# Splitting the second half of the last image pair's load by partitions into 8 and 120, in a 3x3 convolution on one core

## Chip, cores and metric

One core of one Trainium2 chip. The metric is device time in microseconds (us) per execution. The kernel before has a median of 127.45 us over 3 runs (127.39 to 127.47). In the profile, PE is the matrix engine (TensorE), PEld its weight loads, DVE the vector engine, ACT the scalar engine, POOL is GpSimd, SP is the queue that issues the stores and, at the start, the loads of the weights and of the first rows.

## The reference

```
x:      (16, 64, 64, 64) float32       # batch, channels in, rows, columns
weight: (128, 64, 3, 3)  float32       # nine tenths zeros, drawn at random
out[b, co] = sum over ci, kh, kw of weight[co, ci, kh, kw] * x_pad[b, ci, kh:kh+64, kw:kw+64]
```

It is a plain 3x3 convolution with padding 1; the kernel treats the weights as dense.

## The kernel before

The 16 images are taken as 8 pairs: two images of 64 channels fill the 128 partitions. GpSimd loads each pair from memory and casts it to bf16 on the way. SP stores the float32 results.

```python
xs = [x_pool.tile([128, H, W], BF16, name=f"x{p}") for p in range(NP)]      # one tile for each pair
nc.sync.dma_start(out=w_sb, in_=...)                                       # weights, SP's queue
nc.sync.dma_start(out=x_head, in_=pair(0)[:, 0:HEAD, :])                   # first rows of pair 0
nc.gpsimd.dma_start(out=xs[0][:, HEAD:H, :], in_=pair(0)[:, HEAD:H, :])    # load 0 on GpSimd
ident = const_pool.tile([128, 128], BF16, name="ident"); make_identity(nc, ident)
for p in range(1, NP):
    nc.gpsimd.dma_start(out=xs[p], in_=pair(p))                            # loads 1 to 7

for _ in range(27):                                                        # idle matmuls, wake the clock
    nc.tensor.matmul(idle_ps, idle_rhs, idle_rhs, start=True, stop=True)
# ... weights transposed ...

def twos(p, o, r0):                          # 16 rows; needs a sum of row pairs, made on GpSimd
    s = s_pool.tile([128, 8, W], BF16, name="s")
    nc.gpsimd.tensor_tensor(out=s, in0=xs[p][:, r0 : r0 + 16 : 2, :],
                            in1=xs[p][:, r0 + 1 : r0 + 16 : 2, :], op=ADD)
    shared = product([(s, G1, 0, 1)], 8)     # PE, in program order: s first, then x
    # ... even and odd rows: product(...) of xs[p], added to shared on DVE ...

for p in range(NP):
    # ... block 0 of pair 0 goes the direct way (no s), all other blocks through twos ...
    # ... two stores of 2 MB for each pair; four of 1 MB for the last pair ...
```

GpSimd's queue is one sequence. The loads stand on it first, then all the block sums s. PE needs one s for each block, in order.

Of the kernel before, what the change touches and what calls it, by code (L numbers as in the profile page):

```python
# [27 lines left out]
def kernel(  # L28
# [6 lines left out]
    nc = tc.nc  # L35

    B, C_IN, H, W = x.shape
    C_OUT, _, KH, KW = weight.shape
    assert (B, C_IN, H, W) == (16, 64, 64, 64) and (C_OUT, KH, KW) == (128, 3, 3)
    NP = B // 2  # L40
# [14 lines left out]
    def pair(p):  # L55
        return x[2 * p : 2 * p + 2].rearrange("n i h w -> (n i) h w")

    xs = [x_pool.tile([128, H, W], BF16, name=f"x{p}") for p in range(NP)]
# [4 lines left out]
    nc.gpsimd.dma_start(out=xs[0][:, HEAD:H, :], in_=pair(0)[:, HEAD:H, :])  # L63
    ident = const_pool.tile([128, 128], BF16, name="ident")
    make_identity(nc, ident)
    for p in range(1, NP):
        nc.gpsimd.dma_start(out=xs[p], in_=pair(p))  # L67


    idle_rhs = const_pool.tile([128, 128], BF16, name="idle_rhs")  # L70
# [147 lines left out]
```

## Time and profile before

| | before |
|---|---|
| time, median | 127.45 us |
| profiled execution, span | 125.7 us |
| first store issued | 24.06 us |
| pair 6's first store issued | 100.84 us |
| last store: first, median, second last, last of its 16 landings | 121.84, 122.72, 123.76, 124.56 us |

The last two rows come from the trace's records. In the trace each transfer raises its semaphore 16 times, as many times as the core has DMA engines, and the time of every rise is recorded. This text reads each rise as the landing of one engine's share, so one transfer's 16 landings show how far the engines are apart. The records don't carry the engine's number.

The profile's page of the kernel before. The rows of digits cut the span into 40 slices: PE, POOL and DMA are tenths of busy time, PEclk the clock granted to PE.

```profile
span 125.7 us, 2486 instructions
...
PE   6689999999999999999999999999999999990000
...
POOL 6908543333333333333333333333333330000000
PEclk9999999999999999999999999999999999997555
DMA  4999999999999999999999999999999999999980
...
PE 84%; DMA 4%; DVE 1%; issue 1%; DVEq 0%; SPq 0%
```

PE is full in every slice from the fourth until its work ends near 113 us, and DMA from the second slice until the last stores drain. The last line, the chain that ended last, is 84% PE. It ends with DVE's last additions at 114.2 us; what follows is the drain of the stores. Two limits nearly tie: PE feeds the stores, and the DMA engines carry a backlog to the end.

Stages of the kernel before. The columns are busy time of PE, PEld, DVE, ACT and POOL with instruction counts, then granted clock, DMA share and GB/s.

```profile
90.00:100.00 10.00, 10.00 (x96) 5.15 (x94) 7.82 (x13) 3.22 (x6) 3.45 (x3) 1.00 0.99 423
100.00:110.00 10.00, 10.00 (x98) 5.08 (x94) 7.96 (x14) 3.22 (x6) 1.15 (x1) 1.00 1.02 434
110.00:120.00 10.00, 2.86 (x28) 1.27 (x24) 3.48 (x6) 1.07 (x2) 0.00 (x0) 0.75 0.98 410
```

DMA has no room left. The start, as a timeline of the kernel before (start, duration, engine, line, operation; in brackets the idle time before it and what ended it):

```profile
6.68 6.89 PE L134 MATMUL ps<-x,wT 64*128 64x512 bf16 x36 [1.21 <-DVE x L87]
10.00 3.37 POOL L153 TENSOR_TENSOR s<-x 128x512 bf16<-128x512 bf16 x3 [3.81 <-DMA x<-in_x_dram]
13.39 0.82 PE L134 MATMUL ps<-s,wT 64*128 64x512 bf16 x6
```

GpSimd starts the sums at 10.00 us, just after load 0's last landing (9.86 us). PE reaches the first product of s at 13.39 us and finds it ready: no bracket, so no wait.

### The profile page before, as it was taken

The numbers are of one execution on the slowest core, as the hardware profiler recorded it, in microseconds if no ns is written. First come the engines' busy times: TensorE is split into PE (matmuls) and PEld (weight loads), VectorE is DVE, ScalarE is ACT, GpSimd is POOL, SyncE is SP. The second block draws the span as 40 slices with busy tenths as digits, with TensorE's granted clock in tenths as the row PEclk, the third lists the DMA queues.
The fourth block names the chain that finished last, engine by engine and source line by source line (L and its number), as shares of the span: only waits on it lengthen the run. The fifth ranks groups of instructions, "written<-read, shape, count | busy, mean of one in ns | idle before, by whom it ended". The sixth has DMA issues, their size and how long they took to land.

```text
span 125.7 us, 2486 instructions
## 1 busy us (share of the span) xinstructions
PE 110.5 (88%) x1002; PEld 57.5 (46%) x1002; DVE 82.2 (65%) x135; ACT 38.1 (30%) x70; POOL 40.7 (32%) x45
## 2 busy tenths in 40 slices
PE   6689999999999999999999999999999999990000
PEld 6434555555555455545554555555555555540000
DVE  0452277788878787877787778777877787773000
ACT  4511533333333333332433333333333333330000
POOL 6908543333333333333333333333333330000000
PEclk9999999999999999999999999999999999997555
DMA  4999999999999999999999999999999999999980
GB/s 116 254 220 214 219 216 216 214 203 334 313 292 334 334 302 344 323 318 352 412 435 433 433 433 422 417 438 425 443 422 422 412 438 427 448 396 407 422 362 21
DMA packets 4044, 42.70 MB, mean 340 GB/s; under 512 B 448, under 2 KB 448, under 8 KB 832
## 3 DMA queue, kind: packets, MB, share of 16 engines
q1 hardware_dynamic: 2880, 34.44, 65.6%
q0 software_dynamic: 1152, 8.09, 31.3%
q8 instruction: 8, 0.13, 0.4%
q14 instruction: 4, 0.03, 0.1%
HBM read 17.07 MB, written 33.55 MB: 403 GB/s over the span
## 4 chain that ended last, share of the span: by engine, by line
PE 84%; DMA 4%; DVE 1%; issue 1%; DVEq 0%; SPq 0%
PE ps L134 84%; DMA x_head<-in_x_dram 4%; DVE o L167 1%; DVEq L213 0%; DVE x L87 0%; SPq L60 0%; DVEq L167 0%
## 5 line engine op out<-in xcount | busy, mean ns | idle before, releaser
L134 PE MATMUL ps<-x,wT 64*128 64x504 bf16 (+3 forms) x780 | 91.5, 382 | 1.2 <-DVE x L87 1.2
L167 DVE TENSOR_TENSOR o<-ps,pc 128x512 f32<-128x512 f32 x124 | 77.8, 685 | 22.1 <-PE ps L134 19.8
L134 PEld LDWEIGHTS <-wT 64*128 64x128 bf16 x966 | 53.9, 96 | 53.3 <-issue 4.5
L153 POOL TENSOR_TENSOR s<-x 128x512 bf16<-128x512 bf16 x31 | 35.6, 1151 | 60.2 <-PE ps L134 42.9
L160 ACT COPY pc<-ps 128x512 f32<-128x512 f32 x62 | 33.3, 589 | 64.0 <-issue 61.8
L134 PE MATMUL ps<-s,wT 64*128 64x512 bf16 (+1 forms) x186 | 25.6, 377 | 0.0
L148 DVE COPY o<-ps 128x512 f32<-128x512 f32 x2 | 1.4, 691 | 4.9 <-PE ps L134 4.9
L74 PE MATMUL ps<-idle_rhs 128*128 128x128 bf16 x27 | 3.1, 313 | 1.0 <-DVE idle_rhs L71 1.0
L67 POOL DMA_DIRECT2D x<-in_x_dram x7 | 3.7, 561 | 0.0
L74 PEld LDWEIGHTS <-idle_rhs 128*128 128x128 bf16 x27 | 2.8, 148 | 1.0 <-DVE idle_rhs L71 1.0
L147 ACT COPY o<-ps 128x512 f32<-128x512 f32 x2 | 1.2, 586 | 6.2 <-PE ps L134 6.2
L91 DVE CAST w_bf<-w_sb 128x192 bf16<-128x192 f32 (+1 forms) x4 | 1.1, 353 | 2.8 <-DMA w_sb<-in_weight_dram 2.8
L91 ACT ACT_TABLE_LOAD x1 | 1.3, 1283 | 0.7 <-PEq L202 0.7
L97 PE MATMUL ps<-ident,w_bf 128*128 128x128 bf16 x9 | 1.2, 309 | 0.2 <-DVE w_bf L91 0.2
L87 DVE CAST x<-x_head 128x576 bf16<-128x576 f32 x1 | 0.5, 459 | 1.3 <-DMA x_head<-in_x_dram 1.3
L91 ACT CAST w_bf<-w_sb 128x64 bf16<-128x64 f32 (+1 forms) x2 | 0.7, 420 | 1.7 <-DMA w_sb<-in_weight_dram 1.7
L97 PEld LDWEIGHTS <-w_bf 128*128 128x128 bf16 x9 | 0.8, 129 | 0.6 <-DVE w_bf L91 0.6
L101 DVE TENSOR_TENSOR wT<-ps,wT 128x384 bf16<-128x384 f32 x2 | 1.0, 546 | 0.0
L63 POOL DMA_DIRECT2D x<-in_x_dram x1 | 0.7, 696 | 0.8 <-POOLq L202 0.8
L87 ACT CAST x<-x_head 128x576 bf16<-128x576 f32 x1 | 0.7, 672 | 0.2 <-DMA x_head<-in_x_dram 0.2
L71 DVE MEMSET idle_rhs<- 128x64 uint32 x1 | 0.1, 112 | 0.8 <-PEq L202 0.8
L110 ACT CAST wT<-ps 128x384 bf16<-128x384 f32 x1 | 0.5, 478 | 0.4 <-PE ps L97 0.4
(8 smaller groups left out, 1.9 us busy)
## 6 DMA issues: line engine op xcount, KB each, us to landing
out_dram<-o SPq DMA_DIRECT2D x14, 2048.0 KB, 17.9
x<-in_x_dram POOLq DMA_DIRECT2D x7, 1024.0 KB, 29.9
out_dram<-o SPq DMA_DIRECT2D x4, 1024.0 KB, 10.2
x<-in_x_dram POOLq DMA_DIRECT2D x1, 736.0 KB, 8.6
x_head<-in_x_dram SPq DMA_DIRECT2D x1, 576.0 KB, 5.0
w_sb<-in_weight_dram SPq DMA_DIRECT2D x1, 288.0 KB, 2.9
```

The costliest lines, as they stand in the source:

```text
L67: nc.gpsimd.dma_start(out=xs[p], in_=pair(p))
L74: nc.tensor.matmul(idle_ps, idle_rhs, idle_rhs, start=True, stop=True)
L87: copy(out=xs[0][:, a:b, :], in_=x_head[:, a:b, :])
L91: copy(out=w_bf4[:, g, a:b, :], in_=w_v[:, k : k + b - a, :])
L97: nc.tensor.matmul(wps[:, j, :], src, ident, start=True, stop=True)
L101: nc.vector.tensor_tensor(out=wT[:, g], in0=wps, in1=wT[:, G1], op=SUB)
L134: nc.tensor.matmul(ps[n][:, lo:hi, c_lo:c_hi], tap(g, kw, n), src[q, a:b:step, c_lo + kw - 1 : c_hi + kw - 1], start=(i == 0), stop=(i == ...
L147: nc.scalar.copy(out=o[0][:, r0 : r0 + rows, :], in_=ps[0])
L148: nc.vector.tensor_copy(out=o[1][:, r0 : r0 + rows, :], in_=ps[1])
L153: nc.gpsimd.tensor_tensor(out=s, in0=xs[p][:, r0 : r0 + 16 : 2, :], in1=xs[p][:, r0 + 1 : r0 + 16 : 2, :], op=ADD)
L160: nc.scalar.copy(out=c, in_=shared[n])
L167: nc.vector.tensor_tensor(out=o[n][:, first : r0 + 16 : 2, :], in0=ps[n], in1=pc[n], op=ADD)
```

## The change

Its intent: one DMA engine should carry less of the last load. By the rule that the prediction cites, and if the rotation stands at engine 0, the 8 rows should fall on eight engines (0 to 7) and the 120 rows on fifteen (all but 7). An engine that lags would then catch up.

```diff
-    for p in range(1, NP):
+    for p in range(1, NP - 1):
         nc.gpsimd.dma_start(out=xs[p], in_=pair(p))
+    p = NP - 1
+    nc.gpsimd.dma_start(out=xs[p][:, 0 : H // 2, :], in_=pair(p)[:, 0 : H // 2, :])
+    for a, b in ((0, 8), (8, 128)):
+        nc.gpsimd.dma_start(out=xs[p][a:b, H // 2 : H, :], in_=pair(p)[a:b, H // 2 : H, :])
```

## The prediction

> **What bounds the kernel now.** Two things nearly tie. The page has PE busy 110.5 us of a 125.7 us span; the chain of waits is PE from 6.7 to 111.7 us with no wait in it. The stage windows have the DMA share at 0.97 to 1.03 from 10 to 120 us. The semaphore records give each transfer's 16 landings. The last store lands on one engine at 121.84, on the second slowest at 123.76, on the slowest at 124.56 us. That straggler arises among the loads (pair 5: fifteen landings by 50.08, the last at 53.51) and is carried to the end; the store phase keeps the spread near 2.7 us. So slow engine's DMA ends the kernel, while the fast engines are fed just in time by PE: pair 6's first store is issued at 100.84 us, when pair 5's last store lands at 101.80 (fastest) to 104.51 (slowest).
>
> **What the change intends.** The Trainium skill, "DMA: Bandwidth & Descriptors", section "Why a DMA increments its semaphore by 16 and not by 1", says k engines divide the slowest dimension and that GpSimd's k<16 copies start at a rotating cursor: 8 rows on engines 0-7, 120 rows on 15 engines from engine 8. A full load alone lands every 4.87 us, so half a load is 2.4 us per engine: engine 7 would lose about 2.1 us, engines 0-6 gain 0.3. If engine 7 is the straggler, the second slowest engine ends it instead: worth at most 0.5 to 0.8 us (0.5%). No trace yet shows which engine is slow.
>
> **What it adds.** GpSimd's loads go from 8 to 10, and the program has 8 semaphores for them. The built order of instructions shows it: the 8-row load waits for load 0 to land, the 120-row load for pair 1 to land. Both stand on GpSimd's queue before all the block sums s. Before: load 0 lands at 9.86, sums run 10.00 to 13.37, and PE takes the first sum at 13.39. After: GpSimd is held until pair 1 lands at 14.72, issues (0.56 us), and ends its first sum (1.15 us) near 16.6. PE, in order, stands idle from 13.4 to 16.6: about 3.2 us, all on PE's chain, which has no slack to recover it.
>
> **Clock.** The granted clock rose at 12.6 and fell at 115.0 us, only 2 us after the last matmul; 102.4 us is 30 windows of 3.413 us, the window named in the skill's "TensorE: Matmul & The Clock Gate". A window 37% busy was thus enough to lose the clock. A 3.2 us hole probably (65%) drops it; matmul pairs then cost 0.43 instead of 0.22 us for one or two windows: another 1.5 to 3.2 us.
>
> **Sum.** PE's delay d is 3.2, 4.7 or 6.3 us. Pair 6's stores then reach empty engines, so all end near 121.84 + d, plus about 0.6 of spread, against 124.56: +1.1, +2.6 or +4.2 us. The balance gained on engine 7 is swallowed. Predicted 129.9 us, 80% range 127.9 to 132.0. Chances: faster by over 2% 0.01, within 2% 0.51, slower 0.48.
>
> **What would show it.** PE's wait for GpSimd's s of about 3 us near 13.4 us (absent before); GpSimd's wait for DMA until about 14.8 instead of 10.0; granted clock at half in a window near 16 to 23 us; the first store issued 3 to 6 us after 24.06; DMA share below 1 around 100 to 107 us; smaller spread of the last landings, near 1 us; last landing at 125.7 to 128.8.
>
> **What would make it wrong.** The clock holding through the hole (then about 128.5); the fast engines having more backlog than the landings suggest, hiding more of d; pair 1 landing earlier; the 8- and 120-row issues costing GpSimd much more than 0.56 us each; the rotating choice sparing another engine (little matters then).

## The result and the profile after

Ratios here are the mean time of one kernel's fast runs over that of the other's fast runs of the same rounds, so not quite the ratio of the medians.

| | before | after |
|---|---|---|
| time, median of 4 | 127.46 us (127.39 to 127.74) | 132.21 us (131.66 to 133.14) |
| ratio, 95% interval | | 1.0376 (1.0307 to 1.0445) |
| first store issued | 24.06 us | 30.02 us |
| pair 6's first store issued | 100.84 us | 106.79 us |
| last store: first, median, second last, last landing | 121.84, 122.72, 123.76, 124.56 | 127.80, 127.91, 128.71, 129.71 |

The kernel is slower by 3.8%. Those lines of the page, after:

```profile
span 130.9 us, 2488 instructions
...
PE   6592099999999999999999999999999999993000
...
POOL 6901490333333333333333333333333330000000
PEclk9999855999999999999999999999999999999555
DMA  4999999999999999999999999999399929989990
...
PE 77%; DMA 9%; POOL 2%; issue 1%; DVE 1%; DVEq 0%; POOLq 0%
```

PE now has a hole around its fifth slice, the granted clock is down in slices five to seven, and DMA has gaps late in the kernel. The chain now holds DMA (9%) and POOL. Stages after:

```profile
90.00:98.00 8.00, 8.00 (x80) 4.13 (x76) 6.36 (x11) 3.08 (x6) 3.14 (x3) 1.00 0.76 319
98.00:108.00 10.00, 10.00 (x98) 5.14 (x96) 7.57 (x13) 3.37 (x7) 3.77 (x4) 1.00 0.71 298
108.00:118.00 10.00, 10.00 (x96) 5.05 (x94) 7.82 (x13) 3.22 (x6) 0.00 (x0) 1.00 1.00 419
```

The DMA engines wait for work between 90 and 108 us, while PE is fully busy: PE is now late and sets the pace. The start of the kernel after:

```profile
6.58 3.99 PE L138 MATMUL ps<-x,wT 64*128 64x512 bf16 x36 [1.13 <-ACT x L91]
9.84 0.52 POOL L71 DMA_DIRECT2D x<-in_x_dram  x1 [3.60 <-DMA x<-in_x_dram]
14.71 0.53 POOL L71 DMA_DIRECT2D x<-in_x_dram  x1 [4.35 <-DMA x<-in_x_dram]
15.26 4.46 POOL L157 TENSOR_TENSOR s<-x 128x512 bf16<-128x512 bf16 x4
16.47 1.47 PE L138 MATMUL ps<-s,wT 64*128 64x512 bf16 x6 [5.91 <-POOL s L157]
17.70 5.06 PE L138 MATMUL ps<-x,wT 64*128 64x512 bf16 x24
22.58 0.82 PE L138 MATMUL ps<-s,wT 64*128 64x512 bf16 x6
```

Read it from the second line on. GpSimd waits for load 0 and issues the 8 rows at 9.84 us, waits 4.35 us for pair 1's load and issues the 120 rows at 14.71, and only then starts the sums. PE stands idle for 5.91 us. It then runs slowly: from one s product to the next takes 22.58 - 16.47 = 6.11 us here, and took 16.63 - 13.39 = 3.24 us before. The reason for the waits is in the built program: eight semaphores serve GpSimd's loads, the program now has ten loads, and the ninth and tenth reuse the first two semaphores and wait for them. (The trace agrees: the semaphores of load 0 and of pair 1 have 32 rises each, where before they had 16.) GpSimd's built instruction order, not timed:

```
before: L67 load x7 ...                      L153 sum s (pair 0) [waits load 0] ...
after:  L67 load x6, L69 half                (eight loads by here)
        L71  8 rows   [waits DMASW0: load 0 has landed]
        L71 120 rows  [waits DMASW1: pair 1 has landed]
        L157 sum s (pair 0) ...
```

The first store's delay is then a sum: 16.47 - 13.39 = 3.08 us because PE starts the block late, and 6.11 - 3.24 = 2.87 us from the slow clock, together 5.95; measured 30.02 - 24.06 = 5.96. It is never recovered, because PE has no other wait to give up: pair 6's store is 5.95 us late, and the earliest landing of the last store is 127.80 - 121.84 = 5.96 us late. The last landing is less late, 5.15 us, because the backlog of the slower engines is gone.

The clock records give the rest. Before, the clock rose at 12.60 us and fell at 115.00. After, it had risen by 5.26 us, fell at 15.50, rose again at 22.33: two windows of 3.41 us at half clock. In the window before the fall (12.09 to 15.50) PE did nothing; in the next (15.50 to 18.91) it worked 72% of the time, and the clock stayed down through one more. The early rise lets PE finish the direct block in 3.99 instead of 6.89 us and arrive at the hole at about 10.6 us.

### The profile page after: what moved, and what is told of

Same layout as the page of the kernel before. It is cut to its first block, busy times and chain, and to the rows that moved or that the text cites. A ratio compares the mean times of both kernels' runs of the same rounds, so it can differ in the third digit from the quotient of the medians.

```text
span 130.9 us, 2488 instructions
## 1 busy us (share of the span) xinstructions
PE 110.6 (84%) x1002; PEld 57.3 (44%) x1002; DVE 82.5 (63%) x135; ACT 38.1 (29%) x70; POOL 41.7 (32%) x47
## 4 chain that ended last, share of the span: by engine, by line
PE 77%; DMA 9%; POOL 2%; issue 1%; DVE 1%; DVEq 0%; POOLq 0%
PE ps L138 77%; DMA x<-in_x_dram 9%; DVE o L171 1%; POOL s L157 1%; POOL x L63 1%; DVEq L217 0%; POOL x L71 0%; POOL ident masks.py:199 0%; POOL ident masks.py:197 0%; POOLq masks.py:199 0%; POOLq L206 0%; DVEq L171 0%
## 5 line engine op out<-in xcount | busy, mean ns | idle before, releaser
L138 PE MATMUL ps<-s,wT 64*128 64x512 bf16 (+1 forms) x186 | 26.2, 384 | 5.9 <-POOL s L157 5.9
L71 POOL DMA_DIRECT2D x<-in_x_dram x2 | 1.1, 526 | 8.0 <-DMA x<-in_x_dram 8.0
L67 POOL DMA_DIRECT2D x<-in_x_dram x6 | 3.2, 559 | 0.0
L63 POOL DMA_DIRECT2D x<-in_x_dram x1 | 0.7, 707 | 0.8 <-POOLq L206 0.8
## 6 DMA issues: line engine op xcount, KB each, us to landing
out_dram<-o SPq DMA_DIRECT2D x14, 2048.0 KB, 13.4
```

The costliest lines, as they stand in the source:

```text
L138: nc.tensor.matmul(ps[n][:, lo:hi, c_lo:c_hi], tap(g, kw, n), src[q, a:b:step, c_lo + kw - 1 : c_hi + kw - 1], start=(i == 0), stop=(i == ...
```

## The experiments

Theory A: the loss is GpSimd's two waits ahead of the first sum, with the clock lost in the hole. Rival B: the uneven split itself costs DMA time. A second question is why the balance brings nothing. Theory S says that a fixed engine is the slow one; theory F says that the straggler is an engine that carried a 16 KB instruction fetch late.

### e1_late_issue: the same loads, behind pair 0's sums

```diff
-    (the three loads of the last pair, issued with the others)
+        if p == 0:      # in the main loop, after pair 0's blocks
+            q = NP - 1
+            nc.gpsimd.dma_start(out=xs[q][:, 0 : H // 2, :], in_=pair(q)[:, 0 : H // 2, :])
+            for a, b in ((0, 8), (8, 128)):
+                nc.gpsimd.dma_start(out=xs[q][a:b, H // 2 : H, :], in_=pair(q)[a:b, H // 2 : H, :])
```

> The same three loads of the last pair (half, 8 rows, 120 rows), but issued on GpSimd after pair 0's three block sums, so that no sum stands behind their waits. Theory A (the cost of the change is GpSimd's two waits ahead of the first sum): PE's 5.9 us wait for s disappears, the clock does not drop near 15 us, and the time is 126.7 to 127.5 us, i.e. that of the kernel before or up to 0.6% less. Rival B (the uneven split itself costs DMA time, for instance by small or filler descriptors): still above 130 us with no hole in PE's work.

Measured: 127.50 us (127.36 to 127.56, 6 runs), ratio 0.9981 (0.9935 to 1.0028). The timeline of e1:

```profile
9.58 3.36 POOL L153 TENSOR_TENSOR s<-x 128x512 bf16<-128x512 bf16 x3 [3.87 <-DMA x<-in_x_dram]
11.96 0.82 PE L134 MATMUL ps<-s,wT 64*128 64x512 bf16 x6
...
12.88 0.57 POOL L187 DMA_DIRECT2D x<-in_x_dram  x1
13.45 0.52 POOL L189 DMA_DIRECT2D x<-in_x_dram  x1
14.58 0.53 POOL L189 DMA_DIRECT2D x<-in_x_dram  x1 [0.62 <-DMA x<-in_x_dram]
```

The sums come first again, PE has no hole, and the clock doesn't drop. The whole loss is gone with the split still there, so rival B falls. Nor is there a gain. One engine now leads: the last store's landings begin at 120.65 and 121.81 us, where the kernel before has 121.84 and 121.93. But the last two are 123.33 and 124.56, against 123.76 and 124.56: the last is where it was. The split did lighten one engine, and it was not the one that ends the kernel.

### e2_rows_3_parts: the same waits without a split by partitions

```diff
-    nc.gpsimd.dma_start(out=xs[p][:, 0 : H // 2, :], in_=pair(p)[:, 0 : H // 2, :])
-    for a, b in ((0, 8), (8, 128)):
-        nc.gpsimd.dma_start(out=xs[p][a:b, H // 2 : H, :], in_=pair(p)[a:b, H // 2 : H, :])
+    for a, b in ((0, 32), (32, 34), (34, 64)):
+        nc.gpsimd.dma_start(out=xs[p][:, a:b, :], in_=pair(p)[:, a:b, :])
```

> No split by partitions: the last pair's load cut by image rows into 32, 2 and 30, all over 128 partitions, ten loads issued up front, so the same two waits and the same bytes in each part. Theory A: as slow as the change, 131 to 133 us, with PE waiting 3 to 6 us for the first s and the first store at 28 to 31 us. Rival B: back to 127 to 128 us, as the balanced split takes the uneven split's cost away.

Measured: 131.89 us (130.16 to 132.49, 4 runs), ratio 1.0241 (1.0153 to 1.0329). Two of the four runs (132.38 and 132.49) count as slow, over 1.5% above the fastest, so the ratio rests on 131.41 and 130.16 alone: slower, but whether by more than 2% is unclear. First store at 28.78 us. Its timeline:

```profile
14.73 0.53 POOL L70 DMA_DIRECT2D x<-in_x_dram  x1 [4.35 <-DMA x<-in_x_dram]
15.27 4.46 POOL L156 TENSOR_TENSOR s<-x 128x512 bf16<-128x512 bf16 x4
16.48 1.46 PE L137 MATMUL ps<-s,wT 64*128 64x512 bf16 x6 [4.47 <-POOL s L156]
17.72 3.80 PE L137 MATMUL ps<-x,wT 64*128 64x512 bf16 x24
21.35 0.82 PE L137 MATMUL ps<-s,wT 64*128 64x512 bf16 x6
```

With every part over 128 partitions, GpSimd is held to the same moment (14.73 us), and the kernel is slow. So the number of loads and their place on the queue make the loss, not their shape. In the profiled execution the clock rose at 9.57 us, so PE came to the hole later (12.0 us), the hole was 4.5 us, and the clock was down for one window (16.40 to 19.81) instead of two. Here too exactly one window (12.98 to 16.40) was empty of PE work. What differs is the next one: PE restarted at its very beginning, worked 98% of it, and the clock rose at its end. The first store was 4.72 us late instead of 5.96. The phase of the clock, which differs from run to run, would explain why the runs of the kernels with a hole scatter over 1.5 to 2.3 us; only one execution of each kernel was traced, so this isn't shown.

### e3_nine_loads: one wait instead of two

```diff
-    for a, b in ((0, 32), (32, 34), (34, 64)):     # as in e2
+    for a, b in ((0, 32), (32, 64)):
```

> The last pair's load in two halves over 128 partitions: nine loads, so only the wait for load 0 (landed at about 9.6 us) stands ahead of the sums, not the one for pair 1 (14.4 us). Theory A says that it is the second wait that costs: the first sum is done at about 11.6 us instead of 16.4, PE waits 0 to 1.1 us for it depending on when the clock rises, time 127.2 to 128.2 us. If any extra load costs by itself, about 129 to 130 us.

Measured: 127.35 us (127.19 to 127.55, 4 runs), ratio 0.9973 (0.9920 to 1.0026). Its first sum, in PE's timeline:

```profile
11.77 0.82 PE L137 MATMUL ps<-s,wT 64*128 64x512 bf16 x6 [1.17 <-POOL s L156]
```

PE waited 1.2 us for s, with an early clock (risen by 5.07 us), and the first store was out at 22.44 us. The wait for load 0 costs nothing, because the first sum needs load 0 anyway. The wait for pair 1 is the costly one.

### e4_filled_hole: the change with PE kept busy

```diff
+                fill_ps = psum_pool.tile([128, 128], FP32, name="ps")     # after pair 0's direct block
+                for _ in range(80):
+                    nc.tensor.matmul(fill_ps, idle_rhs, idle_rhs, start=True, stop=True)
```

> The change, with 80 idle matmuls (56 ns each warm, 4.5 us) after pair 0's direct block, so that PE is busy in the hole while GpSimd is held. Theory: of the 5.95 us by which the first store is late, about 3 are the first sum's lateness and about 3 the two half-clock windows that the hole brings on. With the filler the clock should stay at full speed once risen, the first store be issued 3.1 to 4.5 us after the 24.06 of the kernel before, and the time be 128 to 130.5 us, 2 to 4 us under the change's 132.2. If the clock's loss is not due to the hole, or costs nothing, the time stays at 131.5 to 133 us or grows.

Measured: 129.68 us (129.02 to 130.03, 4 runs), ratio 1.0149 (1.0090 to 1.0207): slower than before, though whether by 2% is unclear. Its page and timeline:

```profile
PEclk9999999999999999999999999999999999999855
...
10.25 4.64 PE L187 MATMUL ps<-idle_rhs 128*128 128x128 bf16 x80
14.47 0.53 POOL L71 DMA_DIRECT2D x<-in_x_dram  x1 [4.34 <-DMA x<-in_x_dram]
15.02 4.48 POOL L157 TENSOR_TENSOR s<-x 128x512 bf16<-128x512 bf16 x4
16.23 0.82 PE L138 MATMUL ps<-s,wT 64*128 64x512 bf16 x6 [1.34 <-POOL s L157]
...
19.47 0.83 PE L138 MATMUL ps<-s,wT 64*128 64x512 bf16 x6
```

The first block starts at the same time as in the change (16.23 against 16.47 us), but takes 3.24 us instead of 6.11: the clock stayed up. The first store is 2.84 us late instead of 5.96. So useless work made the kernel 2.5 us faster (132.21 - 129.68, from different rounds), and the loss is about half lateness of the sum, half clock.

### e5_late_120_first, e6_late_halves, e8_late_spare_3: other engines spared, and none

Edits to e1: the order `(0, 120), (120, 128)` in e5; one part of 128 rows in e6; the parts `(0, 4), (4, 124), (124, 128)` in e8.

> As e1_late_issue, but the 120-row part is issued before the 8-row part, so that the rotating choice should spare another engine (15 in place of 7, if it starts at 0). In e1 one engine led the others by about 2.5 us in the last stores and the last landing (1.2 us after the second) stayed: the engine spared was not the one that ends the kernel. Theory S (one fixed engine is slow, and it is 15): the last store's slowest landing falls to within 0.4 us of the second and the time to 126.3 to 127.0 us. Theory F (the straggler is whichever engine happens to carry a 16 KB instruction fetch late, about 2 us each): time 127.2 to 127.7 us as before, again one engine 2 to 3 us early and one about 1 us late.

> Control for the late issue: the last pair in two halves of 128 rows, the second not split by partitions, issued late as in e1. If the uneven split gains or costs anything by itself, this differs from e1's ratio of 0.998 to the kernel before; I expect 0.997 to 1.001, no engine 2 us early, and the last landing again about 1 us after the second.

> As e1_late_issue, but in parts of 4, 120 and 4 rows, which should spare engine 3. Theory F: 127.2 to 127.8 us, no gain, one engine 2 us early. If engine 3 were the straggler: 126.3 to 127.0 us.

| | median | ratio, interval | last store: first, second, second last, last landing |
|---|---|---|---|
| e5 | 127.78 us | 1.0022 (1.0004 to 1.0041) | 121.31, 121.83, 123.59, 125.19 |
| e6 | 127.32 us | 1.0013 (0.9979 to 1.0047) | 121.85, 121.92, 124.00, 125.29 |
| e8 | 127.28 us | 0.9999 (0.9979 to 1.0020) | 120.65, 121.66, 123.55, 124.28 |

Each has 6 runs; one run of e5 (130.21 us) was slow and is left out of its ratio. With an uneven split one engine leads (0.52 us in e5, 1.01 in e8), with none nobody does (0.07 in e6). In all three another engine is 0.7 to 1.6 us behind the next. Three splits, e1's included, did not meet the straggler. If the choice rotates as intended, they spared three different engines, and that speaks against theory S for these three; it doesn't exclude a fixed engine among the others. That they were different engines no trace shows.

### e7_fewer_idle: the change, with one instruction fetch less

```diff
-    idle_rhs = const_pool.tile([128, 128], BF16, name="idle_rhs")
+    idle_rhs = const_pool.tile([128, 256], BF16, name="idle_rhs")
-    for _ in range(27):
-        nc.tensor.matmul(idle_ps, idle_rhs, idle_rhs, start=True, stop=True)
+    for _ in range(14):
+        nc.tensor.matmul(idle_ps, idle_rhs[:, 0:128], idle_rhs, start=True, stop=True)
```

> The change itself, its hole included, but the 27 idle matmuls of 128 columns at the start are 14 of 256 columns: same PE time, 26 fewer PE instructions. Theory F: the eighth 16 KB instruction fetch, which came at 119.40 us between PE's end and the last stores, falls away or moves, and the slowest landing of the last store comes at most 1.2 us after the median one instead of 1.8 (1.9 in the change's profile, 1.73 in e2), at the same lateness of the first store; time 131 to 132.2 us, with the noise of the clock's phase. Rival (the spread of the last landings has another cause): still 1.7 to 2 us.

Measured: 131.52 us (130.69 to 132.53, 4 runs), ratio 1.0326 (1.0280 to 1.0372). The DMA queues from 118.5 us to the end, first in the change:

```profile
q1 hardware_dynamic: 520, 3.74, 72.2%
q8 instruction: 1, 0.02, 0.5%
q14 instruction: 1, 0.01, 0.2%
```

and in e7:

```profile
q1 hardware_dynamic: 545, 3.94, 79.9%
q14 instruction: 1, 0.01, 0.2%
```

The fetch on queue 8, which the change has at 119.40 us, is gone from e7's tail: e7's records have it at 131.36 us, after the span's end at 130.36. The last store's landings show what it did:

| | pair 6's second store: last landing minus median | last store: last minus median |
|---|---|---|
| after | 0.39 us | 1.80 us |
| e2 | 0.40 us | 1.81 us |
| e7 | 0.35 us | 0.80 us |

In the change and in e2 all engines are together until pair 6's second store has landed; then a 16 KB and an 8 KB fetch pass between 117.8 and 119.4 us, and one engine is 1.8 us behind and another about 0.8. Without the 16 KB fetch, 0.8 us is all that is left. So in these tails a 16 KB fetch puts its engine about 1.8 us behind, though its own packet lasts 0.94 us in the trace; in the change's trace three 8 KB store packets around it, to judge by their times on the same engine, took 0.61 to 0.71 us where others took about 0.31. The trace of e4 agrees: its 80 extra matmuls brought the eighth fetch forward to 104.10 us, and there one engine is already 1.86 us behind the next when pair 6's first store lands (111.91 against 110.05). The change has 0.05 there: its seventh fetch (105.32) came before that store was issued (106.79), its eighth after.

In time the intervals of e7 and of the change overlap. The spans of e7's four runs are shorter (130.4, 128.5, 128.9 and 128.7 us, against 130.9, 129.9, 130.0 and 131.3), but part of this is lost again: its times are 2.1 to 2.9 us longer than its spans, the change's 1.7 to 1.8. The moved fetch lies in that stretch after the span; that it causes the loss was not tested.

### e9_before_fewer_idle: the kernel before, with one fetch less

The same edit, made to the kernel before.

> The kernel before with 14 idle matmuls of 256 columns instead of 27 of 128, so 26 fewer PE instructions and one 16 KB instruction fetch less at the end; no other edit. In the kernels without a hole the last engine was already about 1 us behind when pair 6 was stored, after the seventh fetch (97 to 99 us), not after the eighth (111 to 113 us). So theory F expects seven fetches, the same straggler about 1 us behind the second engine, and no gain: 127.1 to 127.6 us, ratio 0.996 to 1.002. If the eighth fetch were what ends the kernel before, 126.4 to 126.9 us.

Measured: 127.45 us (8 runs, 127.20 to 129.66, the slowest left out of the ratio), ratio 0.9992 (0.9973 to 1.0010). The last fetch is not what ends the kernel before, as expected. Its profile is no help on the straggler: it fell on an execution of 129.66 us, in which the first rows' load landed at 10.5 us instead of about 6, so its landings aren't compared with those of the kernel before. The end of that execution does look like e7's: an 8 KB fetch at 117.09 us, no 16 KB one, and the last landing 0.80 us behind the median.

No run beat the kernel before by more than its noise.

## Why the prediction was wrong

Right: the two waits on GpSimd's queue, found in the built order, were called as the cost, and at their place. The first sum was predicted done near 16.6 us and PE started on it at 16.47. The predicted 3.2 us of lateness was 3.08. The clock was expected to fall in the hole, with 65%, and did. The half clock was expected at 16 to 23 us and came at 15.5 to 22.3. The gaps of DMA share around 100 to 107 us are there (0.71). The balance on one engine brought nothing.

Wrong: 129.9 us was forecast, with 132.0 as the upper end, and 132.21 was measured. The mechanism held, and two terms of the sum were too small: the clock's part of the delay d, and the spread of the last landings. They add up: for the forecast of 129.9 the sum needs d = 4.57 us (124.56 + 129.9 - 127.45 - 121.84 - 0.6).

- **The delay d, by 1.39 us (5.96 against 4.57).** The step is "another 1.5 to 3.2 us" for the clock, counted at 65%, after "PE, in order, stands idle from 13.4 to 16.6: about 3.2 us". The lateness of PE's restart was right (3.08). The clock's part, about 1.4 us on average in the forecast (4.57 - 3.2), measured 2.87 us: two windows at half clock, which is near the largest of its three cases (d of 6.3). The forecast took PE's arrival at 13.4 from the one trace of before, and that arrival hangs on when the clock rises: by 5.26 us in the profile after, against 12.60 before. So PE came at 10.6 us, and the hole was 5.9 us long and held a whole window without work. e4 shows that the hole does cause the loss. One empty window cost two windows at half clock in the change and one in e2; the two traces differ in how much of the next window PE worked (72% and 98%), and so in where the windows happened to lie.
- **The spread, by 1.31 us (1.91 against 0.6).** The step is "all end near 121.84 + d, plus about 0.6 of spread". The fast engines did end at 121.84 + 5.96 = 127.80, to the hundredth. But the last landed 1.91 us after the first, because instruction fetches fell between PE's end and the last stores. The forecast had no such term. Only e7 takes it away, to 0.92 us (129.19 - 128.27). It was this term that took the sum past the range: with d = 5.96 and the forecast's own 0.6 of spread the sum is 131.3, below 132.0.

Together 2.70 us over 129.9 give 132.6; the profiled execution took 132.64.

One premise didn't hold either, though the sum didn't need it: "That straggler arises among the loads" and "is carried to the end". The load whose landings the forecast gives (50.08 and 53.51; by the order of the semaphores it is pair 6's, not pair 5's) has its last engine 3.43 us behind the second last. At pair 5's first store this is down to 0.20 us (99.36 against 99.16), and the 0.80 of the last store arises after that.

The Trainium skill, "DMA: Bandwidth & Descriptors", section "Why a DMA increments its semaphore by 16 and not by 1", says that a copy goes to the largest number of engines up to 16 that divides its slowest dimension, so 120 rows to 15 engines, and that on GpSimd copies with fewer than 16 engines rotate. It also names an exception on trn2 for some of GpSimd's direct copies, without saying which: there 100 partitions lie on engines 0 to 14. By an estimate from the same page 120 rows would too, in every order of the parts; then e1, e5 and e8 would all have spared the same engine. The runs agree with one engine spared: a leading engine in e1, e5 and e8, none in e6. Which number it has, and whether it changes between them, can't be read from these traces. What stays open besides: which engine carries each fetch, and so which one would have to be spared. In the kernels without a hole the last engine was already about 1 us behind when pair 6's stores landed, after the seventh fetch (at 97 to 99 us). That this fetch made it so fits, but no run took that fetch away.

## What to carry to other kernels

Count the transfers a queue issues against the semaphores that the program has for them: beyond that number, a load that nobody needs yet waits for an early one and holds up all that stands behind it. Here the ninth cost nothing and the tenth nearly all. Put late loads behind early compute on the same queue, or keep their number down. And before lightening an engine, make sure that it is the one which is last: here the balance was paid for in full and could not have returned more than 0.8 us, the distance to the next engine.

## What the Trainium skill lacked or had wrong

- "DMA: Bandwidth & Descriptors" does not tell of the limit that made the loss, which is one of the built program: it had eight semaphores for GpSimd's loads, and the ninth and tenth load waited for the first and second (GpSimd held until 14.71 us, +4.75 us in the median).
- "DMA: Bandwidth & Descriptors", section "Latency and other measured facts", says that engines 7 and 15 are usually slower in traces. No run here shows it: sparing one engine in three ways, meant to be 7, 15 and 3, left the last landing at 124.28 to 125.19 us against 124.56.
- "Runtime: NRT & Kernel Launch", section "Instruction fetch mechanics", calls the cost of crossing a 16 KiB block of 256 instructions "one DMA tail-bump, mostly hidden". The size agrees: between fetches PE went through 121 to 146 pairs of weight load and matmul in the change (for instance from 365 matmuls begun at the fetch at 50.59 us to 486 at the one at 63.52). The cost is hidden from PE (busy all 10.00 us from 98 to 108 us, around the fetch at 105.32), but not from the stores that share the DMA engine: with the fetch among the last stores one engine was 1.8 us behind the median, without it 0.8 us (e7).
- "TensorE: Matmul & The Clock Gate", section "What's actually happening", has the clock fall after at least one idle window of about 3.4 us, and the window free-running. The free running agrees: the first rise came between 3.7 and 12.6 us in the profiled fast executions. The idle window is too strict: before, the clock fell at 115.00 us, when the last matmul had ended at about 112.9, so in a window that was 37% busy. The other traces narrow it down: the clock also fell after windows in which PE was busy 35% (e5, at 7.09 us) and 29% (e6, at 7.34), and held through one of 43% (e8, 110.0 to 113.4). It rose after windows that were 79% busy (e5, at 3.68, and e6, at 10.75) and not after one of 74% (the kernel before, 5.77 to 9.19).
